# Input projections of a hybrid encoder block: a third of the weight tiles is split into two parts by loads and ScalarE alone

## The chip, the cores and the metric

The kernel runs on one core of a Trainium2 chip. A core has a matrix engine (TensorE, PE in the profile), a vector engine (VectorE, DVE), an activation engine (ScalarE, ACT), a general engine (GpSimd, POOL) and SyncE (SP), which here only issues transfers. Sixteen DMA engines move data between the memory outside (HBM) and the on-chip SBUF. Each engine works through its own queue of instructions in order and waits on semaphores. The metric is the device time of one execution in microseconds, and the median of several runs is given.

## The reference

One encoder block on x of 256 tokens by 2048 channels, in float32. All input projections come from one matrix, w_in, of 2048 by 12800:

```python
proj = jnp.einsum('bsd,dc->bsc', h, w_in)
lru_x, conv_x, conv_bg, conv_cg, g_lru, g_conv = jnp.split(proj, SPLIT_POINTS, axis=-1)
u = centred_dwconv(lru_x, lru_conv_w, lru_conv_b, LRU_CONV_LEFT)
h_fwd = rg_lru_direction(u, ...)      # sigmoid gates by head, then a linear scan over the tokens
h_bwd = rg_lru_direction(u, ..., True)
y_lru = jnp.einsum('bsw,wd->bsd', h_fwd + h_bwd, w_lru_out)
v = centred_dwconv(conv_cg * conv_x, sc_conv_w, sc_conv_b, SHORT_CONV_LEFT)
y_conv = jnp.einsum('bsc,cd->bsd', conv_bg * v, w_conv_out)
merged = jax.nn.sigmoid(g_lru) * y_lru + jax.nn.sigmoid(g_conv) * y_conv
```

The merged result goes through w_o, a residual and a layer norm, then through an MLP with squared ReLU (8192 wide) and a second layer norm.

## The kernel before

**Products in two parts.** Float32 values are split into a high part `hi`, with the mantissa that one pass of TensorE carries, and a low part `lo = raw - hi`. A product of a weight block with the activations is then two matmuls (`mm_blocks`, L137 and L138): `hi` against both parts of the activations (512 columns), and `lo` against their high part (256 columns). `split` (L64) makes the parts: ScalarE copies `raw` into `hi` with a cast to float32r (L66), and VectorE subtracts (L67). All callers of `split` share these two lines, so the profile keeps them apart by the tile's name.

**The stream of weights.** All weight tiles, mostly 128 x 1024 floats (512 KB), go through one stream in the order of their use (class `Weights`, L70). `load` (L82) starts the transfer of a tile on SP's queue into one of 3 `raw` slots (L85) and splits it into one of 6 `hi` and one of 6 `lo` slots. `take` hands out the next tile, and first loads ahead until the tile five places further on is in the stream (`AHEAD = 5`, `BUFS = 6`). So tile i+5 gets the slot of tile i-1.

**The order of the work.** The first stage, the input projections for the recurrence (names `l<head>`) and the short convolution (names `c<part>_<j>`), runs over 20 heads. For each head come two tiles `l` (the 16 blocks of 128 input channels for one block of 128 outputs), a smaller tile `g` of 256 KB with the gates of the head before (`gate_job`), and four to six tiles `c`. A first group `b` of six tiles runs while x is still arriving. Tiles of one kind follow each other as jobs: a job's products, then what is done with the products of the job before (`post`). These posts are ScalarE's copies of one half (L215), VectorE's sum (L218), the convolutions on VectorE (L258, L260, L345, L347), and for the gates ScalarE's sigmoids (L287) and a product on GpSimd (L289). Every second head runs `recur`: exponentials on ScalarE, squares on GpSimd (L309), and products and two scans for each head on VectorE (L310 to L321). After this stage come the mixers' gates (`sg`), the output projections (`yl`, `yc`), `o`, and the MLP (`f`, `d`), with the same stream.

Tile dependencies are turned into semaphore waits by the framework. Its planner fixes the order of each engine's queue when the kernel is built, by the order of the code and by when it expects operands to be ready. GpSimd issues no transfers of weights; its only transfers (constants and a copy of x, L397, L406, L494) lie in later stages.

Of the kernel before, what the change touches and what calls it, by code (L numbers as in the profile page):

```python
# [8 lines left out]
F32 = mybir.dt.float32  # L9
F32R = mybir.dt.float32r  # L10
AF = mybir.ActivationFunctionType
ALU = mybir.AluOpType
# [3 lines left out]
T = 256  # L16
# [21 lines left out]


class Job:  # L40
    """Weights' tiles that are taken from the stream, the products with them, and what is done with the products."""

    def __init__(self, specs, mm, post, chained=False):
        self.specs, self.mm, self.post, self.chained = specs, mm, post, chained
# [3 lines left out]
def block_kernel(ctx: ExitStack, tc: tile.TileContext, xT, x, par, w_in, w_gate, w_lru, w_conv, w_o, w1, w2,  # L48
                 ln1_g, ln1_b, b2, ln2_g, ln2_b, out):
    nc = tc.nc  # L50
# [7 lines left out]
    def bank_a(name):  # L58
        return psa.tile([P, 512], F32, tag="a", name=name)

    def bank_b(name):
        return psb.tile([P, 512], F32, tag="b", name=name)

    def split(raw, hi, lo):  # L64
        """raw = hi + lo, each with the mantissa that one pass of TensorE carries."""
        made = nc.scalar.copy(hi, raw)  # L66
        nc.vector.tensor_tensor(lo, raw, hi.bitcast(F32), op=ALU.subtract)  # L67
        return made

    class Weights:  # L70
        """All weights' tiles in the order of their use, loaded and split some tiles ahead of it."""

        def __init__(self):
            self.specs, self.tiles, self.taken = [], [], 0

        def alloc(self, name):
            raw = wp.tile([P, CH * P], F32, tag="raw", name=f"raw_{name}", bufs=3)
            hi = wp.tile([P, CH * P], F32R, tag="hi", name=f"hi_{name}", bufs=BUFS)
            lo = wp.tile([P, CH * P], F32R, tag="lo", name=f"lo_{name}", bufs=BUFS)
            return raw, hi, lo  # L80

        def load(self):  # L82
            src, n, name = self.specs[len(self.tiles)]
            raw, hi, lo = self.alloc(name)
            nc.sync.dma_start(raw[:, :n], src)  # L85
            split(raw[:, :n], hi[:, :n], lo[:, :n])
            self.tiles.append((hi, lo))

        def take(self, hold=False):
# [7 lines left out]
    stream = Weights()  # L97
# [5 lines left out]
        return par_sb[:, o : o + 1]  # L103

    def decay_scale():
        """-8 softplus(-lambda), with log1p by a Newton step on expm1(y) = 2 t / (1 - t), t = tanh(y / 2)."""
        n = 2 * HEADS
        o = PCOLS["lam"][0]
        lam = par_sb[:, o : o + n]
        tl = {k: cp.tile([P, n], F32, name=f"sp_{k}") for k in ("e", "y", "t", "r", "q")}  # L110
        e, y, t, r, q = (tl[k] for k in ("e", "y", "t", "r", "q"))
        c = cp.tile([P, n], F32, name="c_neg")
        cpos = cp.tile([P, n], F32, name="c_pos")
        nc.scalar.activation(e, lam, AF.Abs)
        nc.scalar.activation(e, e, AF.Exp, scale=-1.0)
        nc.scalar.activation(y, e, AF.Ln, bias=1.0)
        nc.scalar.activation(t, y, AF.Tanh, scale=0.5)
        nc.vector.tensor_scalar(r, t, -1.0, 1.0, op0=ALU.mult, op1=ALU.add)
        nc.vector.reciprocal(q, r)
        nc.vector.scalar_tensor_tensor(r, t, 2.0, q, op0=ALU.mult, op1=ALU.mult)  # L120
        nc.vector.tensor_tensor(t, r, e, op=ALU.subtract)
        nc.vector.tensor_scalar_add(q, e, 1.0)
        nc.vector.reciprocal(r, q)
        nc.vector.tensor_tensor(q, t, r, op=ALU.mult)
        nc.vector.tensor_tensor(r, y, q, op=ALU.subtract)
        nc.vector.tensor_scalar(t, lam, -1.0, 0.0, op0=ALU.mult, op1=ALU.max)
        nc.vector.tensor_tensor(y, t, r, op=ALU.add)
        nc.vector.tensor_scalar(c, y, -LRU_C, None, op0=ALU.mult)
        nc.vector.tensor_scalar(cpos, y, LRU_C, None, op0=ALU.mult)
        return c, cpos  # L130

    def mm_blocks(ps, hi, lo, k0, k, n, src, w0=0):
        """ps[:, :T] + ps[:, T:] = W.T @ (hi + lo): W's high part meets both parts, its low part the high one."""
        for i in range(k0, k0 + k):
            s = src(i)
            w = slice((i - k0 + w0) * P, (i - k0 + w0 + 1) * P)
            nc.tensor.matmul(ps, hi[:, w], s, start=i == 0, stop=False)  # L137
            nc.tensor.matmul(ps[:, :T], lo[:, w], s[:, :T], start=False, stop=i == n - 1)  # L138
# [12 lines left out]
        return Job(specs, mm, lambda: post(st["ps"]))  # L151

    def group_job(w, cs, nk, src, posts, name, after=None):
        """Some blocks of columns side by side, so that products can begin while their second operand is in the making."""
        st = {}
        cuts = [(k0, min(CH, nk - k0)) for k0 in range(0, nk, CH)]
        specs = [(w[c, :, k0 : k0 + k, :].rearrange("p k q -> p (k q)"), k * P, f"{name}{c}_{k0}") for k0, k in cuts for c in cs]

        def mm():
            st["ps"] = [bank_a(f"ps_{name}{c}") for c in cs]  # L160
            for k0, k in cuts:
                with tc.issue_after(after().ins) if after else nullcontext():
                    tiles = [stream.take() for _ in cs]
                for i in range(k):
                    for ps, (hi, lo) in zip(st["ps"], tiles):
                        mm_blocks(ps, hi, lo, k0 + i, 1, nk, src, i)

        def post():
            for ps, p in zip(st["ps"], posts):
                p(ps)  # L170

        return Job(specs, mm, post)

    def row_job(w, nk, src, post, name, tail=0, between=None):
        """Products with tokens on the output's partitions; over the last tiles one half of the tokens after the other."""
        st = {}
        n = nk // 2
        specs = [(w[i], 2 * 512, f"{name}_{i}") for i in range(n)]

        def products(ps, i, t, hi, lo):  # L180
            for kk in range(2):
                k = 2 * i + kk
                s = src(k)
                c = slice(kk * 512, (kk + 1) * 512)
                sh = s[:, t * P : (t + 1) * P]
                sl = s[:, T + t * P : T + (t + 1) * P]
                nc.tensor.matmul(ps[t], sh, hi[:, c], start=k == 0, stop=False)  # L187
                nc.tensor.matmul(ps[t], sh, lo[:, c], start=False, stop=False)  # L188
                nc.tensor.matmul(ps[t], sl, hi[:, c], start=False, stop=k == nk - 1)  # L189

        def mm():
            ps = st["ps"] = [bank_b(f"pr_{name}_{t}") for t in range(2)]
            for i in range(n - tail):
                hi, lo = stream.take()
                for t in range(2):
                    products(ps, i, t, hi, lo)
            last = [stream.take(between is not None and i > 2) for i in range(tail)]
            for t in range(2):
                for i, (hi, lo) in enumerate(last):
                    if t and between and i == tail - 1:  # L200
                        between()
                    products(ps, n - tail + i, t, hi, lo)
                if tail and not t:
                    post(ps[0], 0)

        def finish():
            for t in range(1 if tail else 0, 2):
                post(st["ps"][t], t)

        return Job(specs, mm, finish, chained=True)  # L210
# [13 lines left out]
        scope[name] = es = ExitStack()  # L224
        return es.enter_context(tc.tile_pool(name=name, bufs=1, reuse_waits="tile"))

    # x, channels on partitions, with the first weights among its parts
    xraw = sp.tile([P, KD, T], F32, tag="s0", name="xraw")
    xs = sp.tile([P, KD, 2 * T], F32R, tag="s1", name="xs")
    xsrc = lambda k: xs[:, k, :]  # L230
# [91 lines left out]
            d = hsrc(h)  # L322
            split(y[:, 0, :], d[:, :T], d[:, T:])

    # short convolution
    conv = {}
    cpads = []
    for i in range(2):
# [25 lines left out]
                split(s, conv["cs"][:, j, :T], conv["cs"][:, j, T:])  # L354
        return post

    # gates of the two mixers
    sg = {}

    def gate_sig_post(i):  # L360
# [6 lines left out]
            nc.scalar.activation(sg["s"][:, i, :], s, AF.Sigmoid)  # L367
        return post

    # the two mixers' outputs, merged  # L370
    mgd = {}

    def merge_post(j, part):
# [64 lines left out]
        return post  # L438

    def first_norm(t):  # L440
        """The normalized rows' transposes, scaled and shifted by channel, as the next products' second operand."""
        zp, z = zd["p"], zd["z"]
        if "hsp" not in zd:
            zd["hsp"] = sp.tile([P, KD, 2 * T], F32R, tag="s0", name="hsp")
# [1 line left out]
        for q in range(4):  # L446
            ps = (bank_b if t else bank_a)(f"tr{t}_{q}")
# [3 lines left out]
            for i in (0, 2):  # L451
# [5 lines left out]
                hi = hsp[:, js, t * P : (t + 1) * P]  # L457
# [72 lines left out]
    done = 2  # L530
    for h in range(HEADS):
# [7 lines left out]
        done = upto  # L539
# [7 lines left out]
    for c in range(4):  # L547
        jobs.append(row_job(w_o[c], KD, lambda k: mgd["m"][:, k, :], wo_post(c), f"o{c}", tail=5 if c == 3 else 0,
                            between=(lambda: first_norm(0)) if c == 3 else None))
    for half in range(2):  # L550
        f0 = half * HALF
        if not half:
            first = group_job(w1, list(range(3)), KD, lambda k: zd["hsp"][:, k, :], [ff_post(f) for f in range(3)], "f",
                              after=lambda: zd["normed"])
# [9 lines left out]
    for job in jobs:  # L564
        stream.specs += job.specs

    # the first tiles in small parts, x's among them
    cut = (2, 2, 4)
    first = [stream.alloc(s[2]) for s in stream.specs[:3]]
    k0 = 0  # L570
# [79 lines left out]
```

## Time and profile before

| | |
|---|---|
| median of 3 runs | 1651.99 us (1651.96 to 1653.0) |
| profiled execution, first to last instruction | 1649.8 us |
| TensorE busy | 1614.6 us |
| VectorE busy | 1064.8 us |
| ScalarE busy | 847.3 us |
| GpSimd busy | 64.2 us |
| moved by DMA | 312.05 MB, mean 189 GB/s |
| input projections after the first group | 30.2 to 435.6 us |

The span is that of one profiled execution. A busy time counts the time in which at least one instruction of the engine was under way, without transfers being issued. In the rows of the profile, L67 is line 67 of the kernel, `out<-in` gives the tiles by the program's names without numbers, `x91` is a count, and after the bar stand the busy time, the mean ns of one instruction, and the idle time just before them with what ended it. A line such as `PE a <- DVE b` in the view of waits means that TensorE stood idle before an instruction that writes a until VectorE had written b. `SPq` is SP's queue of transfers.

### The profile page before, as it was taken

The page shows a single profiled execution, that of the slowest core. Times are in us where ns is not written, and L with a number is a line of the kernel's source. Part 1 is how long each engine was busy: PE and PEld are TensorE (multiplying, and loading weights), DVE is VectorE, ACT ScalarE, POOL GpSimd, SP SyncE. Part 2 cuts the span into 40 slices and gives each one's busy share as a digit, 9 for nine tenths or more (in the row PEclk, how much of TensorE's full clock was granted, in tenths as well). Part 3 has the DMA queues.
Part 4 walks back from the last instruction along what each step waited for, and adds up shares of the span by engine and source line. Part 5 has one row for each costly group of instructions (what it writes and reads, how often), then busy time and mean ns, then how long its engine had stood idle before and what let it go on. Part 6 is the DMA issues. An engine that isn't in the chain of part 4 may idle for free.

```text
span 1649.8 us, 22706 instructions
## 1 busy us (share of the span) xinstructions
PE 1614.6 (98%) x8592; PEld 1375.4 (83%) x8592; DVE 1064.8 (65%) x1437; ACT 847.3 (51%) x1215; POOL 64.2 (4%) x69
## 2 busy tenths in 40 slices
PE   7999999999999999999999899999999999999996
PEld 6888888888888888888888788888888888888885
DVE  5788888888865546666555777654444666654445
ACT  5676776676755544444333645443333445543331
POOL 0111111011100000000000000000000000000001
PEclk9999999999999999999999999999999999999998
DMA  7555555656566656665775556555565565565552
GB/s 231 188 172 187 192 173 185 188 170 190 175 203 204 194 178 186 192 190 181 246 254 167 165 186 202 188 192 183 187 191 184 187 190 189 189 236 191 183 188 89
DMA packets 88652, 312.05 MB, mean 189 GB/s; under 512 B 9824, under 2 KB 10720, under 8 KB 87648
## 3 DMA queue, kind: packets, MB, share of 16 engines
q1 hardware_dynamic: 87264, 302.75, 57.3%
q0 software_dynamic: 992, 7.34, 1.2%
q8 instruction: 67, 1.10, 0.3%
q10 hardware_dynamic: 288, 0.52, 0.1%
q14 instruction: 41, 0.34, 0.1%
HBM read 308.48 MB, written 2.10 MB: 188 GB/s over the span
## 4 chain that ended last, share of the span: by engine, by line
PE 71%; issue 13%; DVE 7%; DMA 4%; ACT 4%; POOL 0%; SPq 0%; ACTq 0%; POOLq 0%
PE ps_f L137 14%; PE ps_f L138 7%; PE ps_sg L137 6%; PE ps_c L137 5%; PE ps_yl L137 4%; PE pr_d L189 4%; PE pr_d L188 4%; PE pr_d L187 4%; PE ps_yc L137 4%; PE ps_sg L138 3%; PE ps_c L138 2%; PE ps_yl L138 2%; PE ps_yc L138 2%; PE ps_l L137 2%; DMA raw_l<-in_w_in 2%
## 5 line engine op out<-in xcount | busy, mean ns | idle before, releaser
L137 PE MATMUL ps_f<-hsp,hi_f 128*128 128x512 f32 x1024 | 358.6, 393 | 1.0 <-DVE hsp L459 1.0
L138 PE MATMUL ps_f<-hsp,lo_f 128*128 128x256 f32 x1024 | 286.4, 280 | 0.0
L67 DVE TENSOR_TENSOR lo_d<-raw_d,hi_d 128x1024 fp32r<-128x1024 f32 x128 | 156.7, 1225 | 183.7 <-ACT hi_d L66 183.7
L137 PE MATMUL ps_c<-xs,hi_c 128*128 128x512 f32 x736 | 259.4, 394 | 0.0
L66 ACT CAST hi_d<-raw_d 128x1024 fp32r<-128x1024 f32 x128 | 134.6, 1052 | 220.0 <-PE pr_d L189 193.8
L137 PEld LDWEIGHTS ps_f<-hsp,hi_f 128*128 128x128 f32 x1024 | 192.0, 187 | 47.2 <-ACT hf L455 1.3
L67 DVE TENSOR_TENSOR lo_f<-raw_f,hi_f 128x1024 fp32r<-128x1024 f32 x128 | 156.2, 1225 | 115.7 <-ACT hi_f L66 114.3
L66 ACT CAST hi_f<-raw_f 128x1024 fp32r<-128x1024 f32 x128 | 134.1, 1051 | 175.1 <-PE ps_f L137 138.9
L138 PE MATMUL ps_c<-xs,lo_c 128*128 128x256 f32 x736 | 207.5, 282 | 6.4 <-DVE lo_c L67 6.2
L189 PE MATMUL pr_d<-hi_d,ff 128*128 128x512 f32 x512 | 203.2, 397 | 0.0
L188 PE MATMUL pr_d<-lo_d,ff 128*128 128x512 f32 x512 | 203.2, 397 | 0.0
L187 PE MATMUL pr_d<-hi_d,ff 128*128 128x512 f32 x512 | 203.2, 397 | 0.0
L138 PEld LDWEIGHTS ps_f<-hsp,lo_f 128*128 128x128 f32 x1024 | 192.2, 188 | 0.0
L137 PE MATMUL ps_sg<-xs,hi_sg 128*128 128x512 f32 x512 | 179.4, 394 | 0.5 <-DVE sg L218 0.5
L137 PEld LDWEIGHTS ps_c<-xs,hi_c 128*128 128x128 f32 x736 | 138.0, 188 | 31.6
L138 PEld LDWEIGHTS ps_c<-xs,lo_c 128*128 128x128 f32 x736 | 138.3, 188 | 10.5 <-DVE lo_c L67 10.5
L138 PE MATMUL ps_sg<-xs,lo_sg 128*128 128x256 f32 x512 | 143.2, 280 | 0.0
L67 DVE TENSOR_TENSOR lo_c<-raw_c,hi_c 128x1024 fp32r<-128x1024 f32 x92 | 114.4, 1245 | 28.2 <-ACT hi_c L66 26.0
L66 ACT CAST hi_c<-raw_c 128x1024 fp32r<-128x1024 f32 x92 | 96.4, 1048 | 67.4 <-DMA raw_c<-in_w_in 63.6
L67 DVE TENSOR_TENSOR lo_sg<-raw_sg,hi_sg 128x1024 fp32r<-128x1024 f32 x64 | 78.7, 1233 | 67.8 <-ACT hi_sg L66 66.3
L189 PEld LDWEIGHTS pr_d<-hi_d,ff 128*128 128x128 f32 x512 | 96.6, 189 | 23.3
L187 PEld LDWEIGHTS pr_d<-hi_d,ff 128*128 128x128 f32 x512 | 96.6, 189 | 23.3
(165 smaller groups left out, 2789.5 us busy)
## 6 DMA issues: line engine op xcount, KB each, us to landing
raw_f<-in_w SPq DMA_DIRECT2D x128, 512.0 KB, 4.3
raw_d<-in_w SPq DMA_DIRECT2D x128, 512.0 KB, 3.3
raw_c<-in_w_in SPq DMA_DIRECT2D x92, 512.0 KB, 4.1
raw_sg<-in_w_in SPq DMA_DIRECT2D x64, 512.0 KB, 4.6
raw_l<-in_w_in SPq DMA_DIRECT2D x38, 512.0 KB, 4.6
raw_yl<-in_w_lru SPq DMA_DIRECT2D x32, 512.0 KB, 4.3
raw_yc<-in_w_conv SPq DMA_DIRECT2D x32, 512.0 KB, 3.8
raw_o<-in_w_o SPq DMA_DIRECT2D x32, 512.0 KB, 4.3
```

Of the source, the lines that this page charges most:

```text
L66: made = nc.scalar.copy(hi, raw)
L67: nc.vector.tensor_tensor(lo, raw, hi.bitcast(F32), op=ALU.subtract)
L137: nc.tensor.matmul(ps, hi[:, w], s, start=i == 0, stop=False)
L138: nc.tensor.matmul(ps[:, :T], lo[:, w], s[:, :T], start=False, stop=i == n - 1)
L187: nc.tensor.matmul(ps[t], sh, hi[:, c], start=k == 0, stop=False)
L188: nc.tensor.matmul(ps[t], sh, lo[:, c], start=False, stop=False)
L189: nc.tensor.matmul(ps[t], sl, hi[:, c], start=False, stop=k == nk - 1)
```

## The change

In the input projections' `l` and `c` tiles, each tile whose number in the stream leaves 1 when divided by 3 takes a new path. No `raw` slot is used. GpSimd issues a load straight from HBM into `hi`, whose type is float32r, so that the transfer casts. ScalarE writes `lo = -hi`. A second load of the same weights, again issued by GpSimd, adds them to `lo` in the transfer, so that `lo = raw - hi` comes about without VectorE. This adding load is not issued at once: `load` keeps it and issues it at its next call, after the split of the next tile. All other tiles, and all other stages, keep the old path. There are 44 such tiles among the 130.

```diff
 class Weights:
         def __init__(self):
-            self.specs, self.tiles, self.taken = [], [], 0
+            self.specs, self.tiles, self.taken, self.rest = [], [], 0, None
 
         def alloc(self, name):
             raw = wp.tile([P, CH * P], F32, tag="raw", name=f"raw_{name}", bufs=3)
+            return raw, *self.alloc_parts(name)
+
+        def alloc_parts(self, name):
             hi = wp.tile([P, CH * P], F32R, tag="hi", name=f"hi_{name}", bufs=BUFS)
             lo = wp.tile([P, CH * P], F32R, tag="lo", name=f"lo_{name}", bufs=BUFS)
-            return raw, hi, lo
+            return hi, lo
 
         def load(self):
             src, n, name = self.specs[len(self.tiles)]
+            rest, self.rest = self.rest, None
+            if name[0] in "cl" and len(self.tiles) % 3 == 1:
+                hi, lo = self.alloc_parts(name)
+                nc.gpsimd.dma_start(hi[:, :n], src)
+                nc.scalar.mul(lo[:, :n], hi[:, :n].bitcast(F32), -1.0)
+                self.rest = lo[:, :n], src
+                self.tiles.append((hi, lo))
+                return
             raw, hi, lo = self.alloc(name)
             nc.sync.dma_start(raw[:, :n], src)
             split(raw[:, :n], hi[:, :n], lo[:, :n])
+            if rest:
+                nc.gpsimd.dma_start(*rest, accum_op=ALU.add)
             self.tiles.append((hi, lo))
```

## The prediction

> **What bounds the kernel now.** First the engines' totals on the profile's page, to see which engine can set the end:
>
> ```profile
> span 1649.8 us, 22706 instructions
> PE 1614.6 (98%) x8592; PEld 1375.4 (83%) x8592; DVE 1064.8 (65%) x1437; ACT 847.3 (51%) x1215; POOL 64.2 (4%) x69
> ```
>
> TensorE is busy for 98% of 1649.8 us. The median of the runs is 1651.99, so 2.2 us lie around the span; I work in the span and add them at the end. Over the whole kernel VectorE (DVE) is no bottleneck at 65%. That share is an average, so next I read the busy times by stage. The change touches only tiles that TensorE uses between 30.2 us (end of the first group) and 435.6 us (last gate product). Columns: window, length, busy time and instructions of PE, PEld, DVE, ACT, POOL, then clock, DMA share and GB/s.
>
> ```profile
> 30.20:435.60 405.40, 397.42 (x2322) 346.31 (x2321) 344.94 (x527) 287.85 (x469) 45.59 (x37) 1.00 0.57 182
> 41.20:119.70 78.50, 78.50 (x466) 69.28 (x465) 62.61 (x101) 54.88 (x89) 9.08 (x7) 1.00 0.58 183
> 48.30:65.10 16.80, 16.80 (x99) 14.66 (x98) 12.56 (x24) 10.56 (x16) 1.30 (x1) 1.00 0.59 186
> 122.50:142.60 20.10, 19.01 (x111) 16.15 (x110) 18.91 (x33) 13.72 (x24) 0.76 (x1) 1.00 0.56 177
> 436.00:796.00 360.00, 359.47 (x2051) 313.18 (x2050) 212.80 (x273) 179.96 (x266) 3.81 (x3) 1.00 0.62 191
> ```
>
> The stage has 130 weight tiles of 16 products and 20 gate tiles of 12, so 2320 products (two more are cut at the window's edges). The second row is a stretch in which TensorE never pauses: 26 weight tiles and 4 gate tiles, 464 products, exactly a fifth of the stage in the same mix. At its pace the stage would take 5 x 78.50 = 392.5 us. It takes 405.4, so **12.9 us of TensorE are lost in this stage**. The granted clock is 1.00 in all rows, so it is not the clock. What is late is told by TensorE's waits in the stage (who waited for whom, us, times, longest):
>
> ```profile
> PE ps_c L138 <- DVE lo_c L67: 6.2, 7, 1.3
> PE pg L280 <- DVE us L67: 1.6, 3, 0.7
> ```
>
> Both name VectorE: the low part of a weight tile is not yet subtracted, or the low part of u. (7.8 of the 12.9 us are such waits; the rest are products spaced wider around them, with no releaser named.) In the disturbed window 122.5 to 142.6 VectorE is busy 18.91 of 20.10 us, 94%; in the undisturbed one 62.61 of 78.50, 80%. So the loss comes in bursts, when the recurrence's scans (L319 to L321) stand in VectorE's queue between two subtractions. After 436 us VectorE is at 59% and TensorE at 359.47 of 360: nothing to gain there. SP says the same, since a raw slot comes free only with VectorE's subtraction, and ScalarE (ACT) waits behind it:
>
> ```profile
> SPq L85 <- DVE lo_c L67: 103.9, 42, 4.5
> SPq L85 <- DVE us L67: 49.9, 16, 4.0
> SPq L85 <- DVE lo_l L67: 42.6, 20, 3.9
> ```
> ```profile
> ACT hi_c L66 <- DMA raw_c<-in_w_in: 59.4, 51, 2.8
> ACT hi_l L66 <- DMA raw_l<-in_w_in: 24.9, 23, 2.8
> ```
>
> **What the change removes.** By the order of the stream 44 of the 130 tiles take the new path (numbers 7, 10, 13, ... whose name begins with c or l). Their costs today:
>
> ```profile
> L67 DVE TENSOR_TENSOR lo_c<-raw_c,hi_c 128x1024 fp32r<-128x1024 f32 x91 | 113.1, 1245 | 26.2 <-ACT hi_c L66 24.0 <-PE ps_c L138 1.1 <-PE ps_l L137 0.7
> L66 ACT CAST hi_c<-raw_c 128x1024 fp32r<-128x1024 f32 x90 | 94.3, 1048 | 63.2 <-DMA raw_c<-in_w_in 59.4 <-PE ps_c L137 1.4 <-PE ps_l L137 1.4
> L287 ACT ACT_TABLE_LOAD x10 | 12.8, 1283 | 0.2
> L309 POOL TENSOR_TENSOR q<-a 128x512 f32<-128x512 f32 x18 | 18.7, 1040 | 35.8 <-ACT a L304 27.9 <-DVE ri L310 7.9
> L289 POOL TENSOR_TENSOR ri<-ri,u 128x512 f32<-128x512 f32 x19 | 26.9, 1414 | 347.6 <-ACT ri L287 327.1 <-DVE u L260 20.5
> ```
>
> VectorE loses 44 x 1.245 = 54.8 us: its share of the stage falls from 344.94 to 290 of 405, 72%. In the burst window 20.1 us hold about 7.2 tiles, a third of them new, so 2.4 x 1.245 = 3.0 us go: 15.9 of 20.1, 79%. That is the 80% at which the second row shows no pause. I therefore count the whole **12.9 us as recoverable**, and zero as its lower bound. ScalarE's negative replaces its cast: the same 128x1024, 1.05 us, no difference in the sum. A third of the tiles leave the three raw slots, so the other 86 get theirs sooner.
>
> **What it adds.** Every new tile costs two 512 KB loads from POOL's queue in place of one on SP's, and a chain in place of one load that ran ahead. Today the raw load needs only a raw slot. Now the casting load writes straight into a hi slot, which is free only when TensorE is through with the tile six before. From then to its use lie five tiles. The third window row gives a tile's time: six tiles in 16.80 us, 2.80 each; the second then gives a gate tile (78.50 - 26 x 2.80) / 4 = 1.43. For 32 of the 44 tiles a gate is among the five: 4 x 2.80 + 1.43 = 12.6 us; for the other 12 it is 14.0; the mean is 13.0. In this time the tile has to go through casting load, negative and adding load. The rows nearest to these (issue rows: KB each, median us from issue to landing; first fence the stage, second 808 to 835 us, where POOL's loads meet SP's; third POOL's time to issue):
>
> ```profile
> raw_c<-in_w_in SPq DMA_DIRECT2D x88, 512.0 KB, 4.1
> raw_l<-in_w_in SPq DMA_DIRECT2D x38, 512.0 KB, 4.6
> raw_g<-in_w_gate SPq DMA_DIRECT2D x20, 256.0 KB, 3.2
> q1 hardware_dynamic: 21560, 73.25, 56.6%
> ```
> ```profile
> raw_o<-in_w_o SPq DMA_DIRECT2D x9, 512.0 KB, 10.1
> cst<-in_ln_g POOLq DMA_DIRECT2D x1, 1024.0 KB, 8.0
> cst<-in_ln_b POOLq DMA_DIRECT2D x1, 1024.0 KB, 11.2
> ```
> ```profile
> 811.09 0.74 POOL L406 DMA_DIRECT2D cst<-in_ln_g  x1 [358.74 <-PE ps_yl L138]
> 811.82 0.53 POOL L406 DMA_DIRECT2D cst<-in_ln_b  x1
> ```
>
> *Casting load.* No row shows a cast in a DMA. Low 3.2 (the 256 KB load), high 8.0 (1024 KB, the first of POOL's three). I take 4.6, the slower of the plain 512 KB loads, since POOL's issue, inside this time, is only 0.5 to 0.7 us. *Negative.* 1.05 us, plus its place in ScalarE's queue: low nothing, high 1.3 (one table load ahead of it). I take 0.7. *Adding load.* No row shows one. Low 4.1, a plain load, if the add costs nothing. High 11.2, POOL's second 1024 KB load. It must fetch two operands per element, the old lo and the weight, so I add one more tile's share of the engines: 73.25 MB took 56.6% of 405.4 us, so 0.524 MB take 1.6 us; 4.6 + 1.6 = 6.2. The sum is **L = 4.6 + 1.05 + 0.7 + 6.2 = 12.55 us against 12.6 or 14.0**: it just fits. Ends: 3.2 + 1.05 + 4.1 = 8.35 and 8.0 + 1.05 + 1.3 + 11.2 = 21.6.
>
> Where L is too long, TensorE stalls at the tile's first low product. The stall of the new tile three before lies inside the same five tiles, and lengthens them, so each pays s = (L - 13.0) / 2, and the stage 44 s. The high end costs 44 x 4.3 = 189 us, less 12.9; the low end costs nothing.
>
> The Trainium skill (Collectives: The Full Stack, "The bandwidth ceiling: the fold count and why AG ≠ RS ≠ AR") holds that an adding transfer is slow for its two source reads, not for the add. It was measured on transfers between cores; no row here shows an adding load. By it the adding load is my 6.2 and L 12.55; by the plain row it would be 4.6 and L 10.95, with no stall at all.
>
> *Load on the DMA engines.* 44 more loads are 23.1 MB on 73.25 MB: 57% becomes 74%, or 92% if every adding load counts twice. It can be felt: where POOL's 1024 KB loads ran, SP's 512 KB loads landed after 10.1 us. SP's own loads have less to do, two tiles in three, with three slots. That is the cover for them; with it gone they become the next thing late.
>
> *Queues.* On POOL the casting load waits for TensorE, the adding load for the negative, and both hold up the gates' multiplications (L289) and squares (L309). VectorE's L310 waits for the squares: some us ten times, against 115 us that VectorE now has free. On ScalarE the negative waits for the casting load, and the casts of the next two tiles, the sigmoids and the half sums wait behind it. ScalarE has 405.4 - 287.85 = 117.6 us free, of which 84.3 are today's waits for raw loads; 1.5 us lost at each negative would be 66 us. I count both queues at nothing beyond the 0.7, and 3 us in all for the tiles that land late by scatter.
>
> **Sum.** -12.9 + 3 = -9.9: span 1639.9, time **1642**.
>
> **Rivals.** *(1) Slower: the adding load is the new bound.* One mechanism, at the first low product of the new tiles (L138, and L137 behind it): adding load landed after hi's slot was free for more than 13 us. Break-even is 44 s = 12.9, s = 0.29, L = 13.6; one more us in the chain is enough. If ScalarE is held for 1.3 us and the adding load takes two whole loads one after the other (9.2), L = 4.6 + 1.05 + 1.3 + 9.2 = 16.2, s = 1.6, +70 - 12.9 = +57: 1709. With L between 14 and 20, 1656 to 1790. For it: two operations that no row prices, DMA engines at up to 92%. Against it: five tiles of time, and loads in the stage whose median is at most 4.6 us. *(2) Within 0.2%: ScalarE takes VectorE's place.* Held at the negative in order, it hands the other tiles' high parts over later, so the bursts still starve TensorE, or as many small stalls come up at new tiles as go at old ones (L about 13.6). 1649 to 1655. For it: ScalarE already waits 84.3 us for loads. Against it: its free 117.6 us. *(3) The casting load copies the weights unrounded, so that the parts are not what they are called:* the same instructions and bytes, so the same 1642; no case of its own.
>
> **Chances.** The forecast, faster, 0.49; rival 1 0.37; rival 2 0.14. A measurement of this kernel tells about 0.2%, 3.3 us, from no change: faster means below 1648.7, slower above 1655.3. The forecast's own range is 1638 (all 12.9 back, and a us) to 1648. The range reaches into rival 1 up to L = 16.1, 1705, which leaves out about a seventh above and a few hundredths below.
>
> **What would show it.** Right: DVE near 290 us in the stage; TensorE's wait for lo_c by L67 gone; the stage about 395 us long; POOL's adding loads landing within 6 to 7 us. Wrong: TensorE waits at L138 for a DMA into lo, 44 times; landings on POOL's queue above 8 us; SP's raw loads above 6 us; ScalarE's idle time before the negative near the whole landing time. After the stage nothing may change.

## The result, and the profile after

The changed kernel takes 1735.25 us (median of 4 runs, 1733.45 to 1740.41) where the kernel before takes 1651.97 (1650.55 to 1653.0). The ratio is 1.0511, with a 95% interval of 1.0494 to 1.0527: **slower by 83 us**, where 10 us faster were forecast. Its profiled execution took 1735.15 us with a span of 1733.3. First the engines' totals and the two big DMA queues (packets, MB, share of 16 engines) on the page of the changed kernel:

```profile
span 1733.3 us, 22744 instructions
PE 1637.8 (94%) x8592; PEld 1389.3 (80%) x8592; DVE 1014.4 (59%) x1393; ACT 845.4 (49%) x1215; POOL 125.8 (7%) x157
q1 hardware_dynamic: 80928, 279.68, 47.9%
q0 software_dynamic: 13664, 53.48, 13.0%
```

VectorE lost 50 us (1064.8 to 1014.4) of the 55 that the subtractions took, and ScalarE kept its load. So the change does what it says. The windows of the changed kernel (the same columns as in the prediction) tell where the time went:

```profile
29.40:516.80 487.40, 417.74 (x2321) 358.01 (x2320) 299.40 (x491) 289.61 (x476) 107.08 (x124) 0.96 0.72 200
516.80:877.00 360.20, 360.20 (x2057) 313.94 (x2056) 208.54 (x267) 177.16 (x262) 3.79 (x3) 1.00 0.58 188
240.00:280.00 40.00, 35.56 (x208) 30.64 (x207) 27.10 (x44) 25.13 (x41) 7.49 (x9) 1.00 0.74 215
440.00:480.00 40.00, 31.60 (x163) 26.84 (x163) 17.86 (x31) 16.84 (x26) 6.15 (x8) 0.87 0.73 204
```

The stage of the input projections grew from 405.4 to 487.4 us, by 82.0, which is nearly the whole difference. After it TensorE runs through, as before. TensorE's waits inside the stage are only these:

```profile
PE ps_c L154 <- DMA lo_c<-in_w_in: 51.4, 28, 4.5
PE ps_l L154 <- DMA lo_l<-in_w_in: 17.5, 9, 4.8
PE ps_c L153 <- DVE pad L234: 0.8, 1, 0.8
```

L154 is the old L138, a tile's first low product. The waits for VectorE (L67) are gone, as forecast. In their place TensorE waits 37 times for the adding load, 68.9 us. The stage's 487.4 us are the 392.5 of an undisturbed pace, 69.7 in which TensorE is idle (487.40 - 417.74, all of it at the 44 new tiles), and 25.2 in which products follow each other at wider distances. Most of this last part is the clock. It was 1.00 in the whole stage before; here eight stretches, 37.5 us in all, are granted half of it (which gives the 0.96 of the first row and the 0.87 of the last). The products in these stretches start 0.43 and 0.21 us apart in place of 0.23 and 0.12, which adds up to some 15 us. The other 10 us lie around the 38 stalls, where the products next to a stall are some 0.26 us wider apart.

Why the adding load is late is read from its issues (median us from issue to landing) and from GpSimd's timeline in a stretch of three new tiles:

```profile
raw_c<-in_w_in SPq DMA_DIRECT2D x61, 512.0 KB, 5.1
hi_c<-in_w_in POOLq DMA_DIRECT2D x31, 512.0 KB, 7.8
lo_c<-in_w_in POOLq DMA_DIRECT2D x31, 512.0 KB, 6.3
hi_l<-in_w_in POOLq DMA_DIRECT2D x13, 512.0 KB, 7.6
lo_l<-in_w_in POOLq DMA_DIRECT2D x13, 512.0 KB, 6.3
```
```profile
105.23 0.86 POOL L102 DMA_DIRECT2D lo_l<-in_w_in  x1 [8.45 <-ACT lo_l L94]
106.93 1.28 POOL L305 TENSOR_TENSOR ri<-ri,u 128x512 f32<-128x512 f32 x1 [0.84 <-ACT ri L303]
108.17 0.59 POOL L93 DMA_DIRECT2D hi_c<-in_w_in  x1
115.67 0.87 POOL L102 DMA_DIRECT2D lo_c<-in_w_in  x1 [6.91 <-ACT lo_c L94]
116.22 0.88 POOL L93 DMA_DIRECT2D hi_c<-in_w_in  x1
125.86 0.86 POOL L102 DMA_DIRECT2D lo_c<-in_w_in  x1 [8.76 <-ACT t_l L231]
```

The adding load lands after 6.3 us, the 6.2 of the forecast. It is the casting load that is slow, 7.8 in place of 4.6. In the timeline GpSimd stands at an adding load until the negative is there, and the next tile's casting load goes out 0.55 us behind it (116.22 after 115.67). The one at 108.17 stood behind a multiplication for the gates (L305); its slot had been free since 104.8. Followed tile by tile through the trace, from the end of the last product of the tile six before (the slot comes free) to the landing of the adding load, the means are:

| us per new tile | slot free to casting load | casting load lands | until ScalarE starts, and its negative | to adding load | adding load lands | sum L | TensorE's gaps at new tiles |
|---|---|---|---|---|---|---|---|
| forecast | 0 | 4.6 | 0.7 + 1.05 | 0 | 6.2 | 12.55 | none |
| changed kernel | 1.29 | 7.27 | 0.26 + 1.06 | 0.32 | 6.38 | 16.56 | 69.7 at 44 |
| no adding load | 0.53 | 4.93 | 1.11 + 1.06 | - | - | - | none |
| second load plain | 1.18 | 6.03 | 0.33 + 1.06 | 0.30 | 5.11 | 14.00 | 28.5 at 44 |
| every sixth tile | 0.23 | 5.47 | 0.36 + 1.06 | 0.30 | 6.62 | 14.05 | 22.6 at 22 |
| order swapped | 0.44 | 5.25 | 0.16 + 1.06 | 4.95 | 7.95 | 19.81 | 121.7 at 44 |

All rows under the changed kernel's belong to the experiments below.

### The profile page after: what moved, and what is told of

It reads as the page before. It is cut to its first block, busy times and chain, and to the rows that moved or that the text cites. A ratio compares the mean times of both kernels' runs of the same rounds, so it can differ in the third digit from the quotient of the medians.

```text
span 1733.3 us, 22744 instructions
## 1 busy us (share of the span) xinstructions
PE 1637.8 (94%) x8592; PEld 1389.3 (80%) x8592; DVE 1014.4 (59%) x1393; ACT 845.4 (49%) x1215; POOL 125.8 (7%) x157
## 4 chain that ended last, share of the span: by engine, by line
PE 60%; issue 24%; DMA 8%; POOL 4%; DVE 2%; ACT 1%; POOLq 0%; SPq 0%; ACTq 0%; DVEq 0%
PE ps_f L153 14%; PE ps_f L154 7%; PE ps_sg L153 7%; PE ps_yl L153 4%; PE ps_sg L154 3%; PE pr_d L203 3%; PE pr_d L205 3%; PE pr_d L204 3%; PE ps_yc L153 3%; DMA hi_c<-in_w_in 3%; DMA hi_l<-in_w_in 2%; PE ps_yl L154 2%; DMA lo_c<-in_w_in 2%; PE ps_yc L154 2%; PE pr_o L205 2%
## 5 line engine op out<-in xcount | busy, mean ns | idle before, releaser
L154 PE MATMUL ps_f<-hsp,lo_f 128*128 128x256 f32 x1024 | 286.7, 280 | 0.0
L153 PE MATMUL ps_c<-xs,hi_c 128*128 128x512 f32 x736 | 270.6, 406 | 0.8 <-DVE pad L234 0.8
L67 DVE TENSOR_TENSOR lo_d<-raw_d,hi_d 128x1024 fp32r<-128x1024 f32 x128 | 156.8, 1225 | 183.6 <-ACT hi_d L66 183.6
L154 PE MATMUL ps_c<-xs,lo_c 128*128 128x256 f32 x736 | 213.9, 291 | 51.4 <-DMA lo_c<-in_w_in 51.4
L67 DVE TENSOR_TENSOR lo_f<-raw_f,hi_f 128x1024 fp32r<-128x1024 f32 x128 | 156.4, 1225 | 117.8 <-ACT hi_f L66 117.6
L154 PEld LDWEIGHTS ps_f<-hsp,lo_f 128*128 128x128 f32 x1024 | 193.0, 188 | 0.0
L154 PEld LDWEIGHTS ps_c<-xs,lo_c 128*128 128x128 f32 x736 | 143.6, 195 | 60.6 <-DMA lo_c<-in_w_in 60.4
L153 PEld LDWEIGHTS ps_c<-xs,hi_c 128*128 128x128 f32 x736 | 143.5, 195 | 33.8 <-DVE pad L234 1.1
L154 PE MATMUL ps_sg<-xs,lo_sg 128*128 128x256 f32 x512 | 142.9, 279 | 0.0
L67 DVE TENSOR_TENSOR lo_sg<-raw_sg,hi_sg 128x1024 fp32r<-128x1024 f32 x64 | 79.0, 1234 | 74.6 <-ACT hi_sg L66 74.6
L204 PEld LDWEIGHTS pr_d<-lo_d,ff 128*128 128x128 f32 x512 | 96.5, 188 | 23.4
L153 PEld LDWEIGHTS ps_sg<-xs,hi_sg 128*128 128x128 f32 x512 | 95.9, 187 | 23.0
```

## The experiments

The theory after the result: the chain of the new tiles is too long, because successive chains meet on GpSimd's queue and in the DMA engines. At TensorE's pace a new tile comes every 7.0 to 8.4 us, and a chain lasts over 12, so one tile's casting load mostly runs beside its predecessor's adding load. Rivals: the adding load is slow by itself, even alone; the casting load is; ScalarE is; the slots are too few. Each of these runs is compared with runs of the kernel before beside it (1651.35 to 1652.86 us). Diffs are against the changed kernel unless said otherwise.

**No adding load.**

```diff
-            if rest:
-                nc.gpsimd.dma_start(*rest, accum_op=ALU.add)
```

> Leaves out the adding loads, so that in the 44 new tiles the low part stays minus the high part. Theory 'collision' (a casting load is slow only because it stands behind the last tile's adding load on GpSimd's queue and ring): the casting load lands after 4 to 5 us instead of 7.7, TensorE has no wait on these tiles, and what VectorE gives up shows undisturbed: 1638 to 1646 us. Theory 'slow by itself' (a casting load takes 7.7 us whatever else runs): the landing stays at 7 to 8 us; the chain is then 7.7 + 1.1 = 8.8 us, within the 13 us of the five tiles, so that the time is also near 1645 us. The landing tells the two apart. If the time stays above 1690 us, both fall, and it is the negatives in ScalarE's queue.

1639.5 us (1638.27 to 1640.45), ratio 0.9923 (0.9907 to 0.994). A window of it from the start of the stage, its casting loads, and its GpSimd queue:

```profile
30.00:423.00 393.00, 393.00 (x2325) 346.45 (x2324) 296.53 (x490) 287.18 (x474) 68.35 (x80) 1.00 0.59 190
```
```profile
hi_c<-in_w_in POOLq DMA_DIRECT2D x31, 512.0 KB, 4.8
hi_l<-in_w_in POOLq DMA_DIRECT2D x13, 512.0 KB, 4.7
```
```profile
q0 software_dynamic: 7328, 30.41, 5.9%
```

TensorE makes the stage's products in 393.0 us without a pause. So the relief of VectorE, together with that of the raw slots, which these tiles no longer use, is worth 12.5 us, as forecast (12.9). Neither the casting loads, which land after 4.8 us (median), nor ScalarE's negatives cost anything. The whole loss, 95.8 us from here to the changed kernel, comes with the adding loads.

**The second load doesn't add.** It overwrites `lo`, so the bytes and the order stay and the addition goes.

```diff
-                nc.gpsimd.dma_start(*rest, accum_op=ALU.add)
+                nc.gpsimd.dma_start(*rest)
```

> The second load writes the weights over the low part and adds nothing: the same bytes from HBM, the same waits and queues, without the read of the old values. Theory 'two operands' (the adding load pays for a second read, 1.6 us of all DMA engines): its landing falls from 6.3 to about 4.7 us, the casting load behind it from 7.7 to about 6, the chain from 16.6 to 13.4 us, and with half of what is over 13.0 paid by each of 44 tiles the time falls to 1650 to 1670 us. Theory 'collision' with an add that costs nothing: nothing changes, 1730 to 1740 us.

1682.07 us (1681.33 to 1684.37), ratio 1.0186 (1.0171 to 1.0201): between the two expectations. Its waits, loads and queue:

```profile
PE ps_c L154 <- DMA lo_c<-in_w_in: 22.0, 14, 3.6
PE ps_l L154 <- DMA lo_l<-in_w_in: 6.0, 5, 2.9
```
```profile
hi_c<-in_w_in POOLq DMA_DIRECT2D x31, 512.0 KB, 5.8
lo_c<-in_w_in POOLq DMA_DIRECT2D x31, 512.0 KB, 4.4
```
```profile
q0 software_dynamic: 13664, 53.48, 10.1%
```

Of the 95.8 us, a second load of any kind costs 42.6 (1682.07 - 1639.5), and that it adds costs 53.2 more. What an adding load takes of the DMA engines follows from the three queue rows: (13.0% x 1733.3 - 5.9% x 1638.7) / 44 = 2.9 us of all 16 engines; the plain second load takes (10.1% x 1679.4 - 5.9% x 1638.7) / 44 = 1.7. The run with SP's raw loads further below, in which GpSimd's queue carries adding loads alone, gives 2.9 as well. Even with a plain second load the casting load takes 6.0 us and waits 1.2 for its issue, against 4.9 and 0.5 with no second load (means).

**Every sixth tile.** 22 new tiles, so that a chain is over before the next begins.

```diff
-            if name[0] in "cl" and len(self.tiles) % 3 == 1:
+            if name[0] in "cl" and len(self.tiles) % 6 == 1:
```

> Every sixth tile in place of every third, 22 or so new tiles, whose chains are 16 us apart and do not meet. Theory 'slow by itself' (the chain of one tile takes 16.6 us of its own): each new tile has all of 16.6 - 13.0 = 3.6 us to pay, since no earlier new tile lengthens its five tiles: 22 x 3.6 = 79 us, less some 6 us of VectorE's relief, about 1724 us. Theory 'collision': casting load 4.5, negative 1.1, adding load 5.5 to 6.3, with issue about 12 us; it fits into 12.6 us, stalls are at most a few tenths a tile, and half of the relief stays: 1642 to 1652 us.

1674.24 us (1670.53 to 1678.04), ratio 1.0136 (1.0113 to 1.016): between the two expectations. Waits and loads:

```profile
PE ps_c L154 <- DMA lo_c<-in_w_in: 20.6, 14, 4.1
PE ps_l L154 <- DMA lo_l<-in_w_in: 1.9, 2, 1.2
```
```profile
hi_c<-in_w_in POOLq DMA_DIRECT2D x16, 512.0 KB, 5.4
lo_c<-in_w_in POOLq DMA_DIRECT2D x16, 512.0 KB, 6.6
```

A lone chain is 14.05 us. That is already a microsecond over the 13.0 of the window, and it costs that microsecond: 22.6 us at 22 tiles, 1.03 each. Chains that meet add 2.5 us (16.56 - 14.05), of which 1.1 lie ahead of the casting load's issue and 1.8 in its landing; the adding load itself is no slower for it. So both the theory and its rival hold, for a part each.

**The adding load at once**, right behind the negative in the code, and not after the next tile's split.

```diff
-                self.rest = lo[:, :n], src
+                nc.gpsimd.dma_start(lo[:, :n], src, accum_op=ALU.add)
```

> The changed kernel with the adding load issued in the code right behind the negative, not kept for the next call. On GpSimd's queue it stands behind its tile's casting load and ahead of the next one either way, so both theories ('queue' and 'DMA engines') expect no change against the changed kernel: 1728 to 1742 us.

1741.74 us (1739.17 to 1744.45), ratio 1.054 (1.0512 to 1.0568), L = 16.90. Holding the issue back is not the loss.

**The raw load by SP, cast by ScalarE.** Only the adding load stays on GpSimd.

```diff
-                hi, lo = self.alloc_parts(name)
-                nc.gpsimd.dma_start(hi[:, :n], src)
+                raw, hi, lo = self.alloc(name)
+                nc.sync.dma_start(raw[:, :n], src)
+                nc.scalar.copy(hi[:, :n], raw[:, :n])
```

> In every third tile the weights come as before by SP's queue into a raw slot, ScalarE casts them to the high part and then writes its negative; only the adding load is left on GpSimd. VectorE is relieved just as much, ScalarE has 44 x 1.05 = 46 us more. Theory 'collision': the loop on GpSimd's queue is gone, the chain from the free slot is two ScalarE steps and one load, about 9 us, no stall at the new tiles: 1638 to 1650 us. Theory 'two operands' or an adding load that is slow by itself: it still fits into 13 us, so near 1650 us. Were ScalarE the next bound (288 + 46 = 334 of 393 us), stalls would come at tiles whose high part is late, and the time would be 1655 us or more.

1703.47 us (1702.04 to 1705.2), ratio 1.0314 (1.0298 to 1.0329). Waits and adding loads:

```profile
PE ps_c L155 <- DMA lo_c<-in_w_in: 32.9, 11, 6.4
PE ps_l L155 <- DMA lo_l<-in_w_in: 8.6, 3, 6.5
```
```profile
lo_c<-in_w_in POOLq DMA_DIRECT2D x31, 512.0 KB, 8.0
```

With the casting load out of the chain I looked for most of the loss to go. A third of it went (32 us). The adding load, now the only load on GpSimd's queue, lands after 8.0 us, and ScalarE begins a new tile 2.9 us after its slot is free (up to 10), since its cast stands in order behind the other tiles' work. L is 13.64, and 14 stalls make 41.5 us. With every sixth tile in this form:

> Raw tile by SP, high part and negative by ScalarE, adding load by GpSimd, in every sixth tile only. In the run with every third tile the chain took 13.6 us on the mean, 8.0 of them the adding load and 2.9 until ScalarE came to the cast, with stalls in bursts. Half as many adding loads leave the DMA engines and ScalarE freer: adding load 6.5 to 7, chain 11.5 to 12.5 us against 12.8: theory 'queue' expects 1645 to 1655 us; if the stalls come with ScalarE's bursts (each new tile that meets one costs 2 to 6 us), 1660 to 1675 us.

1683.67 us (1680.28 to 1686.18), ratio 1.0187 (1.0161 to 1.0213), worse than either expectation. The adding loads land after 7.4 us on average though they are alone, and ScalarE is 3.1 us late. So that a load waits behind another one on GpSimd's queue is not all that makes it slow.

**A seventh slot for the high parts** in this stage (`hi` only), with one more tile loaded ahead, so that a chain has one tile's time more. First the kernel before with that slot, as the control:

```diff
+            slot = n % (BUFS + 1) if n < STAGE else (n - STAGE + 2) % BUFS
...
-            hi = wp.tile([P, CH * P], F32R, tag="hi", name=f"hi_{name}", bufs=BUFS)
+            hi = pool.tile([P, CH * P], F32R, tag=f"hi{slot}", name=f"hi_{name}", bufs=1)
...
-            while not hold and len(self.tiles) < min(len(self.specs), i + 1 + AHEAD):
+            while not hold and len(self.tiles) < min(len(self.specs), i + 1 + AHEAD + (len(self.tiles) < STAGE)):
```

> The kernel before with the same seventh slot, as a control. Its raw slots come free with VectorE's subtractions, so theory 'slots' and theory 'queue' both expect that VectorE's bursts stay: 1645 to 1653 us.

1658.42 us (1656.28 to 1659.41), ratio 1.0035 (1.0023 to 1.0048): the slot by itself costs 6 us, where no change was expected. With it in the changed kernel:

> The changed kernel with a seventh slot for high parts in the stage, and loading one tile further ahead: from the free slot to its use lie six tiles, 15.7 us on the mean in place of 13.0. Theory 'slots' (each chain of 16.6 us starts when its slot is free and has to fit into the tiles between): s = (16.6 - 15.7) / 2 = 0.45 us for each of 44 tiles, 20 us, and no stall long enough to lower the clock: 1655 to 1670 us. Theory 'queue' (on GpSimd a casting load stands behind the adding load of the tile three before, which waits for the negative, which waits for that tile's casting load; a turn of this loop takes 7.3 + 1.1 + 0.3 + 0.9, nearly 10 us, while TensorE needs a new tile every 7.0 to 8.4 us, and every 15 where one is skipped): a slot more changes little, since nothing in the loop waits for it: 1700 to 1735 us.

1718.16 us (1714.74 to 1722.75), ratio 1.0401 (1.038 to 1.0422): 17 us less than the changed kernel, within the range of theory 'queue' and far from that of theory 'slots'. And with every sixth tile:

> Every sixth tile and the seventh slot together. The lone chain took 14.05 us in the run with every sixth tile, over 1 us more than its 12.8; with six tiles, 15.5 us, it fits under both theories ('slots' and 'queue'), since no chain meets another on GpSimd: no stall at new tiles, half of VectorE's relief: 1640 to 1649 us. Were it above 1660 us, the stalls at lone chains would not come from the slots.

1673.04 us (1669.32 to 1675.18), ratio 1.0124 (1.0105 to 1.0142), where under 1650 was expected. The time that the slot gives is taken by the queues. From the slot's coming free to the casting load's issue pass 3.25 us in the first kernel (1.29 without the slot), and L grows from 16.56 to 18.87. In the second they are 1.97, up to 7.2: there the late casting loads stand behind the gates' multiplications and squares on GpSimd, and the negative waits 1.1 us in ScalarE's queue. So slots are not the main thing that is short.

**The order of the two loads swapped.** GpSimd issues the next new tile's casting load ahead of this tile's adding load, so that the casting load needn't wait for the negative. Its core:

```diff
                 hi, lo = self.alloc_parts(name)
-                nc.gpsimd.dma_start(hi[:, :n], src)
+                casting = nc.gpsimd.dma_start(hi[:, :n], src)
                 nc.scalar.mul(lo[:, :n], hi[:, :n].bitcast(F32), -1.0)
-                self.rest = lo[:, :n], src
+                self.add(casting)
+                self.rest = lo[:, :n], src, len(self.tiles) + 3
...
+        def add(self, casting=None):
+            if self.rest:
+                with tc.issue_after(casting.ins) if casting else nullcontext():
+                    nc.gpsimd.dma_start(*self.rest[:2], accum_op=ALU.add)
+            self.rest = None
```

In the expectations, theory 'queue' says that GpSimd's in-order loop over the negative holds TensorE, and theory 'DMA engines' that two loads in flight at once are slow in either order. With six slots, and then with the seventh:

> The same order of the queue with the changed kernel's six slots. The loop is cut here too, but the adding load lands 15.4 to 16 us after the slot came free, against 13.0 us: half of 2.7 us for each of 44 tiles, 59 us, less VectorE's 12.5, with some loss of clock: theory 'queue' 1695 to 1720 us. Theory 'DMA engines': as the changed kernel, 1730 to 1740 us.

> The kernel with the seventh slot for high parts, and on GpSimd's queue each adding load put behind the casting load of the tile three further on instead of ahead of it. The casting load then waits for its slot alone. Theory 'queue' (in the run with the seventh slot it was the loop over the negative that held TensorE): the loop is cut; the adding load goes out once the next casting load is issued, 8.4 us after its own tile's slot came free, and lands 6.4 to 7 us later, 15.4 to 16 us after the slot, against 15.7 us: little is left, 1650 to 1685 us. If the two loads in flight at once are what is slow (theory 'DMA engines'), the order changes nothing: 1705 to 1725 us as with the seventh slot alone.

1820.13 us (1813.8 to 1825.53), ratio 1.1013 (1.0976 to 1.1049), and 1729.03 (1723.9 to 1733.27), ratio 1.0471 (1.0436 to 1.0506): both above the expectations of either theory, the second by only 4 us above that of 'DMA engines'. The loads and a stretch of GpSimd's timeline of the first:

```profile
hi_c<-in_w_in POOLq DMA_DIRECT2D x31, 512.0 KB, 5.2
lo_c<-in_w_in POOLq DMA_DIRECT2D x31, 512.0 KB, 7.8
```
```profile
223.04 0.55 POOL L92 DMA_DIRECT2D hi_c<-in_w_in  x1 [11.58 <-PE ps_l L160]
223.58 0.95 POOL L108 DMA_DIRECT2D lo_c<-in_w_in  x1
```

The swap swaps which load is slow: the casting load now lands after 5.2 us and the adding load, 0.54 us behind it, after 7.8. Whichever goes second pays: the casting load 2 us (7.27 against 5.25), the adding load 1.6 (7.95 against 6.38). The packets of GpSimd's queue in the trace tell why. In 29 pairs of the changed kernel the casting load is issued some 0.6 us behind the adding load. The pair's 256 packets of 4 KB come one load after the other: the first 128 take 388 ns each on the mean, the other 128 take 191. The casting load's first packet starts 4.4 us after its issue, against 1.4 us in the run without adding loads, and from the first packet to the last the 16 DMA engines are 98% busy. With the order swapped it is the adding load whose packets come second, 3.8 us after its issue, against 1.8 with every sixth tile. So the second load stands behind the first one's packets, at engines that are full.

And the swap brings a new wait: by the order on GpSimd the adding load now mostly waits until TensorE is through with the tile three before, 4.95 us from the negative to its issue. From there at most two tiles remain until its use, 5.6 us, while it takes 7.95 to land.

**The subtraction on GpSimd.** Against the kernel before: no further load at all, and the third of the tiles' `lo` is subtracted by GpSimd in VectorE's place.

```diff
-            split(raw[:, :n], hi[:, :n], lo[:, :n])
+            if name[0] in "cl" and len(self.tiles) % 3 == 1:
+                nc.scalar.copy(hi[:, :n], raw[:, :n])
+                nc.gpsimd.tensor_tensor(lo[:, :n], raw[:, :n], hi[:, :n].bitcast(F32), op=ALU.subtract)
+            else:
+                split(raw[:, :n], hi[:, :n], lo[:, :n])
```

> No added transfer at all: in every third tile GpSimd subtracts in VectorE's place, from the raw slot. VectorE is relieved as in the change; on GpSimd a subtraction of 128x1024 takes about twice the 1.3 us of its products of 128x512, 2.6 us, 114 us in all beside the 46 it has. Both theories hold the transfers responsible, so that the relief should show: 1638 to 1648 us. If instead GpSimd's products for the gates come late behind it, or VectorE slows down beside it, 1650 us or more.

1691.98 us (1690.85 to 1693.19), ratio 1.0241 (1.0225 to 1.0256): no way out. Groups of its stage, and the same groups of the kernel before (their lines are four lower; the last of each reads PSUM, the others SBUF alone):

```profile
L88 POOL TENSOR_TENSOR lo_c<-raw_c,hi_c 128x1024 fp32r<-128x1024 f32 x31 | 81.5, 2629 | 168.6 <-ACT hi_c L87 158.4 <-DVE cg L222 10.1
L324 DVE TENSOR_TENSOR_SCAN y<-a,ri 128x256 f32<-128x256 f32 x18 | 18.4, 1023 | 0.0
L357 DVE TENSOR_TENSOR cb<-cb,cx 128x256 f32<-128x256 f32 x15 | 15.9, 1062 | 0.2
L222 DVE TENSOR_TENSOR cx<-ps_c,t_cx 128x256 f32<-128x256 f32 x15 | 6.2, 412 | 0.0
```
```profile
L320 DVE TENSOR_TENSOR_SCAN y<-a,ri 128x256 f32<-128x256 f32 x18 | 12.0, 668 | 0.0
L353 DVE TENSOR_TENSOR cb<-cb,cx 128x256 f32<-128x256 f32 x15 | 6.3, 419 | 0.2
L218 DVE TENSOR_TENSOR cx<-ps_c,t_cx 128x256 f32<-128x256 f32 x15 | 6.3, 419 | 0.0
```

GpSimd takes 2.6 us for a subtraction that takes VectorE 1.2, and VectorE beside it gets slower: 0.67 to 1.02 us for a scan, 0.42 to 1.06 for a product (L357). VectorE is busy for 366.49 us in this stage, more than the 344.94 of before, with 55 us of work fewer. TensorE's largest waits there are for GpSimd's subtractions (12.1 us, 10 times) and for VectorE's (9.2 us, 9 times).

These means mix two cases. Ten of the 15 products of L357 overlap an instruction of GpSimd in time and take 1.38 us; the other five take the 0.42 of before. Of the scans of L324, four overlap and take 2.28 us, 14 don't and take 0.66. The kernel before has this too: 12 of its 20 first taps (L258) overlap GpSimd's multiplication for the gates (L289) and take 1.43 us, the other eight 0.41. So part of VectorE's bursts there is GpSimd's doing, which the prediction did not see.

**VectorE relieved without loads or GpSimd.** Against the kernel before: the first tap of both convolutions (L258, L345) goes to ScalarE. The line of the first of the two:

```diff
-            nc.vector.tensor_scalar(u, pad[:, 0:T], pcol("cw", h), pcol("cb", h), op0=ALU.mult, op1=ALU.add)
+            nc.scalar.activation(u, pad[:, 0:T], AF.Identity, bias=pcol("cb", h), scale=pcol("cw", h))
```

> The kernel before, with no change to its loads: only the first tap of both convolutions (L258, 20 instructions of some 1.0 us, and L345, 15 of some 0.4 us) is moved from VectorE to ScalarE. Everything is computed. It asks whether relief of VectorE alone, with no further transfer, brings back part of the 12.9 us that the stage loses to VectorE; the run without adding loads gave 12.5 us, with 55 us of VectorE's work gone. Theory (VectorE's bursts are the loss, and ScalarE has room for 20 us more): TensorE's waits for VectorE shrink, 1640 to 1648. Rival (ScalarE, which already has 288 us in the stage, hands the high parts over later, so that what VectorE gains is lost again): 1650 to 1660, with TensorE's waits now ending on ScalarE or on a VectorE that was itself late.

1656.18 us (1651.22 to 1662.21, 12 runs), ratio 1.0022 (1.0007 to 1.0038): the rival's time, at the edge of no difference. Its window over the time of the stage before, and TensorE's largest wait in it:

```profile
30.20:435.60 405.40, 394.98 (x2304) 343.98 (x2303) 329.65 (x489) 303.39 (x503) 47.03 (x37) 1.00 0.56 180
```
```profile
PE ps_c L138 <- DVE lo_c L67: 8.9, 9, 1.3
```

The window starts and ends where the stage before did. VectorE is busy for 15 us less in it (329.65 against 344.94), and TensorE waits for it no less (8.9 us against 6.2). VectorE's idle time ahead of its subtractions, until ScalarE has the high part, rose from 39.8 to 48.5 us. Taking work from VectorE and giving it to ScalarE hands the lateness on. That the 12.5 us cannot be had in any way is not shown.

## Why the prediction was wrong

**What held.** The bound of the kernel before and its price: 12.9 us forecast, 12.5 measured without adding loads. VectorE's share, the same ScalarE load, and an unchanged rest of the kernel. The place of rival 1, TensorE at L138 waiting for a load into `lo`, 37 times at 44 tiles. The adding load's own size, 6.2 forecast, 6.38 measured; the Trainium skill's rule of two source reads (Collectives: The Full Stack, "The bandwidth ceiling: the fold count and why AG ≠ RS ≠ AR") goes the same way, with 2.9 us of the DMA engines for an adding load against 1.7 for a plain one. And the formula for a chain that is too long: s = (16.56 - 13.0) / 2 = 1.78, times 44 is 78 us, against 69.7 measured; in the run with every sixth tile, where no other stall lies inside the window, 14.05 - 13.0 = 1.05 against 1.03.

**What failed.** Two terms of the sum for L. The first is the casting load, put at 4.6 us "since POOL's issue, inside this time, is only 0.5 to 0.7 us": it took 7.27 (mean). Without adding loads it takes 4.93. The 2.3 us between come with the adding loads, 0.5 of them even where chains don't meet (5.47 with every sixth tile); the rest comes where its packets stand behind the adding load's. The second is "I count both queues at nothing beyond the 0.7". ScalarE's queue was indeed worth only 0.26. GpSimd's was worth 1.29 us ahead of the casting load and 0.32 ahead of the adding load. Together 2.7 + 1.3 + 0.3 + 0.2 for the adding load - 0.4 for ScalarE make the 4.0 by which L is longer than 12.55. I had priced each load from rows in which it ran alone or ahead. Yet a row that I had quoted showed the loss: of POOL's two 1024 KB loads issued 0.7 us apart, the first landed after 8.0 us and the second after 11.2, and I took the second for no more than an upper end of the adding load. I had also compared L only with the five tiles that it has. I had not compared it with the distance of new tiles: three tiles, 7.0 to 8.4 us. A chain of 12.55 us every 8 us means that for more than half of the time two are under way on one in-order queue, and that could be read from the numbers that I had.

**What was left out.** The clock. Some 15 us of the 83 are TensorE at a lower granted clock (0.96 on average, 0.87 from 440 to 480 us), in eight stretches of 3.4 or 6.8 us, each in or behind a stall of 1.8 us or more. Eleven other stalls of that length have no such stretch behind them. In the run without adding loads, without such stalls, the stage stays at 1.00. The Trainium skill (TensorE: Matmul & The Clock Gate, "Part 1: The HAM clock gate (the "warmup" mystery)") has the clock halved after an idle window of about 3.4 us; the lengths of the stretches here agree, while in five of the eight cases a stall shorter than that was enough (1.8 to 3.3 us).

**The rivals.** Rival 1 came true, at 1735 and not its 1709. Its L of 16.2 was near the 16.56, but by another way: it gave the surplus to the adding load (9.2) and to ScalarE, and the trace puts it in the casting load behind the adding load. It lacked the clock. Rival 2, ScalarE in VectorE's place, didn't come about in the changed kernel. It showed where ScalarE got more work: in the run with the taps, and in those with SP's raw loads, whose new tiles waited some 3 us for ScalarE. Rival 3 has no time of its own, and no run here tests it. The range ended at 1705 since I cut it at L = 16.1 without a term for the clock. Two sums of the prediction are off by a few us: by the formula, L = 16.1 gives 1707, and L from 14 to 20 gives 1661 to 1793, not 1656 to 1790.

## What to carry to other kernels

A chain that has to run between the freeing of a slot and the use of its tile is compared with two lengths: with the time that the slot gives, and with the distance at which chains follow each other. If it is longer than the second, chains share queues and engines, and prices taken from lone instructions are too low. To replace a 1.2 us instruction on an engine with slack by a second transfer that adds in place costs 2.9 us of all DMA engines and over 6 us of latency. No run here shows a case in which that pays.

## What the runs showed of the hardware that was not expected

- A casting load from float32 to float32r lands about as fast as a plain one when nothing stands ahead of it on GpSimd's queue: 4.7 to 4.8 us (median) for 512 KB in the run without adding loads, beside 4.5 to 4.8 for SP's plain loads there. With a plain second load per new tile it takes 6.0, with an adding one 7.3 (means). Two loads that GpSimd issues 0.6 us apart are moved one after the other: the second's first packet started 4.4 us after its issue, against 1.4 for a load alone.
- An adding load with no other load of GpSimd's ahead of it took 7.4 to 8.0 us where SP's raw loads ran at full number, and 6.4 to 6.6 where SP had a third or a sixth of the tiles less. Why is not shown.
- VectorE's instructions with SBUF operands alone became longer where they overlapped one of GpSimd's, the short ones about three times as long (scan L324 0.66 to 2.28 us, product L357 0.42 to 1.38), the subtraction L67 less so (1.22 to 1.48). Those that read PSUM did not change (0.41 to 0.42 us, 16 of them overlapping). The Trainium skill (SBUF — State Buffer, "Who interferes with whom") says that an instruction of VectorE with two SBUF inputs contends with one of GpSimd that reads SBUF; these rows agree and give it a size. Not every group shows it: the other scan (L323) kept its 0.68 us in three overlaps.
- Stalls of 2 to 5 us cost more than themselves: 70 us of waiting brought some 15 us of lower clock with them, and in the run with the swapped order 121.7 us brought some 47 (27 stretches at half clock, 109 us in all).
